# A two-layer hybrid block on one core: the first layer's gates and values in 512-column products, two projections per accumulator in the second, and another order at the beginning

## The chip, the core and the metric

The kernel runs on one core of one Trainium2 chip, in one launch. The metric is device time in microseconds (us), from the start of the program to its end; lower is better. The core has a matrix engine (TensorE, "PE" in the profile, with its weight loads as "PEld"), a vector engine (VectorE, "DVE"), an engine for functions and copies (ScalarE, "ACT"), GpSimd ("POOL") and SyncE ("SP"), from whose queue the loads are issued.

## The reference, cut to what matters

There are 512 latent tokens and 256 context tokens of width 1024, and two layers. Each layer normalises and modulates the tokens, projects them by one wide matrix, and feeds three mixers: a gated linear attention with 4 heads, a gated recurrence with 8 heads, and a windowed attention with 8 query heads. Each mixer has its own SiLU gate. The second layer doesn't update the context, so its queries, gates and merging are needed for the 512 latent tokens alone.

```python
h  = _rms_norm(x, norm_g) * (1.0 + scale) + shift
hc = _rms_norm(ctx, norm_g) * (1.0 + scale_c) + shift_c
(ga_q, ga_k, ga_v, ga_g, ga_lr, hg_q, hg_f, hg_i, hg_g,
 wa_q, wa_k, wa_v, wa_g, mg) = _split_in(jnp.matmul(h, w_in))
...
y_gla = _head_norm_gate(o_gla, gla_norm_g, ga_g)          # ... * silu(ga_g)
y_hg  = _head_norm_gate(o_hg, hgrn_norm_g, hg_g)          # ... * silu(hg_g)
y_att = _window_attention(q, k, v, kc, vc, attn_sink) * jax.nn.silu(wa_g)
x_new = x + gate * _merge((y_gla, y_hg, y_att), mg, w_branch, w_out)
```

## The kernel before, in words

**Data.** Activations stand transposed: 8 chunks of 128 channels (`k` or `kt`) by 768 tokens, the 512 latent ones first (`NL`), then the 256 of the context (`NC`); `NT` is 768. Every fp32 value that a projection reads is held as a rounded part and a rest, `hH[k]` and `hL[k]` for the activations, `WH(i)` and `WL(i)` for a weight block of 128 columns, which lies in a ring of three (`wring`). A projection is the sum of three products per chunk: WH by hH, WH by hL, WL by hH. Each is one matmul instruction, so 8 chunks make 24 matmuls per output piece.

**Projections.** `proj_T` (line 801) gives channels by tokens: 24 matmuls of 512 columns for the latent tokens and, where the context is wanted too, 24 of 256 columns. `proj_V` (line 819) gives tokens by channels for two weight blocks at once: six groups of 128 tokens, 24 matmuls of 256 columns each. Both write an accumulator that `acc()` (line 623) hands out: 128 partitions by 1024 fp32 words, of which there are two, used in turn. A new accumulator can be written when the readers of the one before the last are done. `silu_evac` (line 1339) reads a gate's 768 (or 512) columns with one SiLU on ScalarE; values are copied out 768 columns at a time by ScalarE or VectorE.

**Order.** The program is written out engine by engine by a generator. A plan lists the projections (`make_plan`), and between their matmuls `pace()` (line 694) puts in steps of background work: the recurrences (`rec_head`) and the attention (`att_block`) of heads whose projections are done. Which step comes when is decided by the generator's own running estimate of each engine's time. Background products go to four smaller accumulators (`mx`). Each engine has its instructions in one written order; semaphores join the engines. Most instructions are issued in helpers, so a row's line is the helper's: L533 is a matmul, L549 a transpose by TensorE, L545 a matmul of 32 output rows, L439 an ACT function, L481 and L479 copies on ACT and DVE, L450 a DVE two-operand operation, L466 a DVE operation with a scalar.

**The beginning.** In the first layer (l = 0) `j_start` makes `h` chunk by chunk while the first two projections run. For chunk k there are: `cond_mm(k)` (8 matmuls of 32 output rows that give shift and scale), `cond_cols(k)` (small products on TensorE that turn them into columns, then two small DVE operations), `make_h1(k)` (two DVE operations, then ACT writes `hH[k]`), and `make_h2(k)` (two DVE operations that write `hL[k]`). Round k of the loop issues, in this order: `make_h2(k)`, the first projection's six matmuls, `cond_mm(k + 2)`, the second projection's six, `cond_cols(k + 2)`, `make_h1(k + 2)`, and from round 3 on `split_v()`, which prepares weights of the next projection on ACT and DVE.

Of the kernel before, what the change touches and what calls it, by code (L numbers as in the profile page):

```python
# [18 lines left out]
F32R = mybir.dt.float32r  # L19
# [300 lines left out]
class Emit:  # L320
# [104 lines left out]
    def act(self, out, in_, func, bias=None, scale=None, accum_out=None):  # L425
        want = None
        if func in (AF.Exp, AF.Ln):
            want = COMBINED
        elif func in (AF.Silu, AF.Sigmoid):
            want = str(func)  # L430
        self.table(want)
        kw = {}
        if bias is not None:
            kw['bias'] = bias
        if scale is not None:
            kw['scale'] = scale
        if accum_out is not None:
            kw['accum_out'] = accum_out
        self.nc.scalar.activation(out, in_, func, **kw)  # L439
        self._do('a', 0.833 * self.size(out) + 95 + (90 if accum_out is not None else 0), out, [in_, bias, scale])  # L440
        if accum_out is not None:
            self.written[accum_out.tensor.name] = self.t['a']
            self.writer[accum_out.tensor.name] = 'a'


    def tt(self, out, a, b, op, eng='v'):
        n = self.size(out)
        cost = {'v': 1.04 * n + 65, 'g': 2.25 * n + 100}
        e = eng if eng in cost else self._pick(cost, out, [a, b])
        (self.nc.vector if e == 'v' else self.nc.gpsimd).tensor_tensor(out, a, b, op=op)  # L450
        self._do(e, cost[e], out, [a, b])
# [80 lines left out]
    def mm(self, out, lhsT, rhs, start=True, stop=True):  # L532
        self.nc.tensor.matmul(out, lhsT=lhsT, rhs=rhs, start=start, stop=stop)  # L533
        n = self.size(rhs)
        if rhs.dtype == F32:
            cost = max(1.667 * n + 6, 224)
        elif rhs.dtype == BF16:
            cost = 60
        else:
            cost = max(0.4167 * n + 13.5, 107 if self.size(lhsT) > 64 else 60)  # L540
        self._do('pe', cost, out, [lhsT, rhs])
# [17 lines left out]
def build(nc, tc, A, COL, es, dump=None):  # L559
# [7 lines left out]
    mx_p = es.enter_context(tc.tile_pool(name="mx", bufs=4, space=PSUM))  # L567

    spool = es.enter_context(tc.tile_pool(name="slots", bufs=NSLOT))
    hH = [pool.tile([P, NT], F32R, name=f"hH{k}") for k in range(KT)]  # L570
    hL = [pool.tile([P, NT], F32R, name=f"hL{k}") for k in range(KT)]
    wring = pool.tile([P, NS, 2, KT, P], F32R, name="wring")
    raw_p = es.enter_context(tc.tile_pool(name="raw", bufs=NRAW))
    ncols = A['cols'].shape[1]
# [35 lines left out]
    def ps_tile(kind, p, shape, n):  # L610
        t = p.tile(shape, F32, tag=kind, name=kind)
        names = live[kind]
        if len(names) >= n:
            old = min(names, key=lambda x: E.seq.get(x, 0))
            E.free_at[t.tensor.name] = E.used.get(old, 0.0) + E.FREE
            names.remove(old)
        names.append(t.tensor.name)
        return t

    def mx():  # L620
        return ps_tile('mx', mx_p, [P, 512], 4)

    def acc():
        return ps_tile('acc', acc_p, [P, 1024], 2)


    queue = arena.queue = deque()
# [66 lines left out]
    def pace(slack=SLACK):  # L694
        while max(E.t['v'], E.t['a']) < E.t['pe'] + slack:
            b = first(E.t['pe'] + 50)
            if b is None:
                break
            step(b)
# [81 lines left out]
    def take(n=1):  # L781
        i = pos[0]
        for j in range(at_job[0], i):
            ring_free[j % NS] = E.t['pe'] + E.FREE
        at_job[0] = i
        pos[0] += n
        loads()
        splits(i + n)
        return i
# [5 lines left out]
    def WH(i):  # L795
        return wring[:, i % NS, 1]

    def WL(i):
        return wring[:, i % NS, 0]

    def proj_T(i, xH, xL, ctx, m=P):

        ps = acc()
        E.t['pe'] = max(E.t['pe'], wready[i])
        for t0, n in ((0, NL), (NL, NC)) if ctx else ((0, NL),):
            k = 0
            for kt in range(KT):
                for w, x in ((WH(i), xH), (WH(i), xL), (WL(i), xH)):
                    mm(ps[0:m, t0:t0 + n], w[:, kt, 0:m], x[kt][:, t0:t0 + n],
                       start=(k == 0), stop=(k == 3 * KT - 1))  # L810
                    k += 1
                if kt == 1 and t0 == 0:
                    ahead()
                if kt % 2 == 1:
                    pace()
        pace()
        return ps

    def proj_V(i, evac):

        s = i % NS
        E.t['pe'] = max(E.t['pe'], wready[i + 1])
        wh = wring[:, s:s + 2, 1]
        wl = wring[:, s:s + 2, 0]
        for t in range(6):
            if t % 3 == 0:
                ps = acc()
            k = 0
            for kt in range(KT):
                for x, w in ((hH, wh), (hL, wh), (hH, wl)):  # L830
                    mm(ps[:, 256 * (t % 3):256 * (t % 3 + 1)],
                       x[kt][:, P * t:P * (t + 1)], w[:, :, kt, :],
                       start=(k == 0), stop=(k == 3 * KT - 1))
                    k += 1
            if t == 0:
                ahead()
            if t % 3 == 2:
                evac(t // 3, ps)
            pace()


# [99 lines left out]
    def make_h2(l, k, x, parts=(0, 1)):  # L941

        for j in parts:
            sl = slice(PARTS[j][0], sum(PARTS[j]))
            stt(hL[k][:, sl], x.ap[:, sl], ada[l][:, k, j:j + 1], hH[k][:, sl].bitcast(F32), ALU.add, ALU.subtract)
        if 1 in parts:
            x.free()
# [388 lines left out]
        finish()  # L1336


    def silu_evac(ps, n):
        b = arena.alloc(n)  # L1340
        act(b.ap, ps[:, 0:n], AF.Silu)
        return b

    def tok(bufs, w, c, o=0, r=False):
        b = bufs[c // 3]
        return (b.r if r else b.ap)[:, 256 * (c % 3) + o:256 * (c % 3) + o + w]
# [28 lines left out]
    def j_start(l, arg):  # L1375
# [36 lines left out]
        def cond_mm(k):  # L1412


            w = stage[k]
            ps = mx()
            for kt in range(KT):
                j = kt % 4
                E.mm4(ps[32 * j:32 * j + 32, 0:2 * P], cs32[:, kt], w[kt // 3].ap[:, 256 * (kt % 3):256 * (kt % 3 + 1)],
                      start=(kt < 4), stop=(kt >= 4))  # L1420
            stage[k] = r = arena.alloc(NT)
            copy(r.ap[:, 0:2 * P], ps[:, 0:2 * P], eng='va', psum=True)
            for b in w:
                b.free()
# [38 lines left out]
        def products(kt, of=(0, 1), js=(0, 1)):  # L1463
            E.t['pe'] = max(E.t['pe'], wready[i + 1])
            for j in js:
                for w, x in ((WH(i + j), hH), (WH(i + j), hL), (WL(i + j), hH)):
                    for t0, n in parts[j]:
                        if (t0 > 0) not in of:
                            continue
                        c = count[j][t0 > 0]  # L1470
                        mm(ps[j][:, t0:t0 + n], w[:, kt], x[kt][:, t0:t0 + n], start=(c == 0), stop=(c == 3 * KT - 1))
                        count[j][t0 > 0] += 1

        count = [[0, 0], [0, 0]]
        if l == 0:

            for k in range(KT):
                make_h2(l, k, xs[k])
                if k == 1:
                    load_rest()  # L1480
                if k == KT - 1:
                    ahead()
                products(k, js=(0,))
                if k + 2 < KT:
                    cond_mm(k + 2)
                products(k, js=(1,))
                if k + 2 < KT:
                    cond_cols(k + 2)
                    make_h1(l, k + 2, xs[k + 2], rs)
                if k >= 3 and raw_v:  # L1490
                    split_v()
        else:

            tail = S0.pop('tail')
            for part in range(2):
                make_h1(l, 0, xs[0], rs, (part,))
                if part == 0:
                    tail[0]()
                for k in range(KT):
                    if k + 1 < KT:  # L1500
                        make_h1(l, k + 1, xs[k + 1], rs, (part,))
                    make_h2(l, k, xs[k], (part,))
                    if part and k == KT - 1:
                        ahead()
                    products(k, (part,))
                    if part == 0 and k in (0, 2):
                        tail[1 + k // 2]()
# [63 lines left out]

    def j_v(l, h):
        S_['v'][h] = vb = [arena.alloc(NT) for _ in range(2)]
        proj_V(take(2), lambda j, ps: copy(vb[j].ap, ps[:, 0:NT], eng='va', psum=True))

    def j_gq(l, h):
        ps = proj_T(take(), hH, hL, S_['ctx'])
# [1 line left out]
        act(qb.ap, ps[:, 0:S_['nt']], AF.Copy, scale=float(128 ** -0.5))  # L1579

    def j_g(l, key):
        ps = proj_T(take(), hH, hL, S_['ctx'])
        S_['g'][key] = silu_evac(ps, S_['nt'])

    def j_grun(l, h):
        q, k, vb = S_['q'].pop(h), S_['k'].pop(h), S_['v'].pop(h)
# [272 lines left out]
```

## Time and profile before

| | |
|---|---|
| median of 3 runs | 2699.06 us (2696.78 to 2701.8) |
| the profiled execution: time | 2699.6 us |
| the profiled execution: span, first to last instruction | 2697.8 us |
| TensorE busy | 2617.0 us, 97% of the span |
| weight loads, VectorE, ScalarE, GpSimd busy | 86%, 66%, 41%, 6% |
| mean granted TensorE clock | 0.991 of full speed |
| DMA | 227.68 MB, 84 GB/s over the span |

TensorE is busy nearly all the time, so its own instructions and the few places where it waits make the time. What the other engines do counts only where TensorE waits for them.

### The profile page before, as it was taken

How to read it: one execution, taken by the hardware profiler on the slowest of the kernel's cores; microseconds unless marked ns; L12 is line 12 of the kernel's file. 1: busy time of each engine (PE TensorE's matmuls, PEld its weight loads, DVE VectorE, ACT ScalarE, POOL GpSimd, SP SyncE). 2: the span in 40 equal slices, each digit the busy share in tenths (PEclk: the TensorE clock that was granted, in tenths of full speed). 3: DMA queues.
4: the chain of work that ended last, by engine and by line, in shares of the span. 5: the costliest groups of instructions: out<-in, count | busy, mean ns of one | idle time of the engine just before them, and what ended most of it. 6: DMA issues, size and time to landing. Idle time of an engine off the chain costs nothing. (4 is left out here: it accounts for less than half of the span.)

```text
span 2697.8 us, 40579 instructions
## 1 busy us (share of the span) xinstructions
PE 2617.0 (97%) x15982; PEld 2318.4 (86%) x15982; DVE 1767.1 (66%) x3592; ACT 1105.6 (41%) x2037; POOL 168.9 (6%) x426
## 2 busy tenths in 40 slices
PE   6999999999999999999999999999999999999998
PEld 3899988999888889888888898888899797888886
DVE  4466666786877766775556556667887887765454
ACT  3444434443434455411111344444665545563222
POOL 0000002010020100000000000001011110000000
PEclk8999999999999999999999999999999999999999
DMA  6111121111121112463423411112221122224333
GB/s 251 40 50 57 59 67 59 50 52 57 49 66 50 46 57 74 148 204 101 140 95 102 141 55 56 62 63 63 69 65 62 55 75 73 73 87 142 126 125 109
DMA packets 89342, 227.68 MB, mean 84 GB/s; under 512 B 9920, under 2 KB 30912, under 8 KB 89152
## 3 DMA queue, kind: packets, MB, share of 16 engines
q1 hardware_dynamic: 89152, 225.09, 25.3%
q8 instruction: 126, 2.06, 0.3%
q14 instruction: 64, 0.52, 0.1%
HBM read 202.24 MB, written 22.81 MB: 83 GB/s over the span
## 5 line engine op out<-in xcount | busy, mean ns | idle before, releaser
L533 PE MATMUL acc<-hH,wring 128*128 128x512 f32 (+1 forms) x5040 | 1402.9, 357 | 14.9 <-ACT s L439 9.8
L533 PEld LDWEIGHTS acc<-hH,wring 128*128 128x128 f32 x5040 | 897.7, 190 | 143.1 <-ACT s L439 11.6
L533 PE MATMUL acc<-hL,wring 128*128 128x512 f32 (+1 forms) x2520 | 884.8, 352 | 16.9 <-DVE hL L466 16.8
L533 PEld LDWEIGHTS acc<-hL,wring 128*128 128x128 f32 x2520 | 479.1, 190 | 76.9 <-DVE hL L466 20.5
L533 PE MATMUL mx<-s,s 128*128 128x256 f32 (+4 forms) x2576 | 389.5, 299 | 12.9 <-DVE s L513 4.4
L533 PEld LDWEIGHTS mx<-s,s 128*128 128x128 f32 (+1 forms) x2576 | 348.4, 192 | 32.8 <-issue 7.1
L450 DVE TENSOR_TENSOR wring<-raw,wring 128x1024 fp32r<-128x1024 f32 x269 | 330.7, 1235 | 28.2 <-ACT wring L481 19.3
L533 PE MATMUL acc<-s,wring 128*128 128x512 f32 (+1 forms) x1728 | 332.4, 354 | 0.5 <-DVE s L450 0.5
L533 PEld LDWEIGHTS acc<-s,wring 128*128 128x128 f32 x1728 | 285.6, 189 | 46.4 <-DVE s L450 0.9
L439 ACT ACTIVATE s<-s 128x768 f32<-128x768 f32 (+1 forms) x321 | 259.0, 816 | 129.8 <-DVE s L466 83.1
L481 ACT CAST wring<-raw 128x1024 fp32r<-128x1024 f32 x173 | 179.7, 1048 | 276.9 <-PE acc L533 182.9
L533 PE MATMUL acc<-wring,hH 128*128 128x256 f32 x1536 | 286.1, 285 | 0.0
L450 DVE TENSOR_TENSOR s<-s,s 128x768 f32<-128x768 f32 (+5 forms) x279 | 234.0, 855 | 67.0 <-ACT s L439 45.9
L533 PEld LDWEIGHTS acc<-wring,hH 128*128 128x128 f32 x1536 | 242.2, 192 | 0.3
L533 PE MATMUL acc<-wring,hL 128*128 128x256 f32 x768 | 217.2, 283 | 0.0
L450 DVE TENSOR_TENSOR s<-s,fb 128x128 f32<-128x128 f32 (+2 forms) x608 | 183.0, 361 | 0.8
L439 ACT ACTIVATE s<-acc 128x768 f32<-128x768 f32 (+2 forms) x112 | 76.3, 683 | 255.9 <-PE acc L533 236.2
L481 ACT COPY s<-mx 128x256 f32<-128x256 f32 (+2 forms) x190 | 67.4, 379 | 225.8 <-PE mx L533 142.8
L479 DVE CAST wring<-raw 128x1024 fp32r<-128x1024 f32 x103 | 71.6, 695 | 117.5 <-PE acc L533 114.4
L533 PEld LDWEIGHTS acc<-wring,hL 128*128 128x128 f32 x768 | 147.3, 192 | 0.2
L481 ACT COPY s<-acc 128x768 f32<-128x768 f32 (+2 forms) x129 | 87.8, 681 | 101.0 <-PE acc L533 98.9
L549 PE MATMUL mx<-const,s 128*128 128x128 f32 (+1 forms) x732 | 109.1, 275 | 15.7 <-DVE s L450 14.6
(112 smaller groups left out, 2144.8 us busy)
## 6 DMA issues: line engine op xcount, KB each, us to landing
raw<-in_W SPq DMA_DIRECT2D x308, 512.0 KB, 3.8
y<-s SPq DMA_DIRECT2D x80, 128.0 KB, 1.7
s<-y SPq DMA_DIRECT2D x24, 384.0 KB, 6.1
s<-in_xT SPq DMA_DIRECT2D x16, 384.0 KB, 4.0
s<-in_wada SPq DMA_DIRECT2D x16, 384.0 KB, 7.6
s<-y SPq DMA_DIRECT2D x24, 256.0 KB, 4.4
y<-s SPq DMA_DIRECT2D x80, 64.0 KB, 1.6
s<-in_wvl SPq DMA_DIRECT2D x8, 288.0 KB, 6.2
```

The costliest lines, as they stand in the source:

```text
L439: self.nc.scalar.activation(out, in_, func, **kw)
L450: (self.nc.vector if e == 'v' else self.nc.gpsimd).tensor_tensor(out, a, b, op=op)
L479: self.nc.vector.tensor_copy(out, in_)
L481: self.nc.scalar.copy(out, in_)
L533: self.nc.tensor.matmul(out, lhsT=lhsT, rhs=rhs, start=start, stop=stop)
L549: self.nc.tensor.transpose(out, in_, ident)
```

## The change

It has four parts.

1. **Gates of the first layer, context part.** `hH[k]` and `hL[k]` become the two halves of one tile. For the 256 context tokens a gate's projection (24 of them: 8 for each mixer) multiplies WH by both halves in one matmul of 512 columns, and WL by hH in one of 256 columns that adds to the second half of the output. The two halves of the output are added on reading: ACT copies one, DVE adds the other, and SiLU then runs as one call of 512 columns out of the accumulator and one of 256 columns in place.
2. **Values of the first layer.** `proj_V2` does the same for the seven value projections that go by `j_v`: per group of 128 tokens and chunk one matmul of 512 columns (hH by WL and WH of both blocks) and one of 256 (hL by WH). Each of six groups is read by a copy on ACT and an addition on DVE; an accumulator holds two groups, where it held three.
3. **Projections of 512 tokens alone** (all of them in the second layer) take half an accumulator, so two of them share one.
4. **The beginning.** `make_h2(k + 1)` is issued in round k, behind `cond_mm(k + 2)`, ahead of `cond_cols(k + 2)` and `make_h1(k + 2)`.

```diff
-    hH = [pool.tile([P, NT], F32R, name=f"hH{k}") for k in range(KT)]
-    hL = [pool.tile([P, NT], F32R, name=f"hL{k}") for k in range(KT)]
+    hHL = [pool.tile([P, 2, NT], F32R, name=f"h{k}") for k in range(KT)]
+    hH, hL = ([t[:, j] for t in hHL] for j in range(2))
...
+    half = [None, 0]
     def acc():
+        half[1] += 1
         return ps_tile('acc', acc_p, [P, 1024], 2)
+    def acc_bank():
+        t = half[0]
+        if t is not None and half[1] < 2:
+            half[0] = None
+            return t
+        t = acc()
+        half[:] = t[:, NL:2 * NL], 0
+        return t[:, 0:NL]
...
+    def psum2(out, a, b):
+        copy(out, a, eng='a', psum=True)
+        tt(out, out, b, ALU.add)
-    def proj_T(i, xH, xL, ctx, m=P):
-        ps = acc()
+    def proj_T(i, xH, xL, ctx, xHL=None):
+        ps = acc() if ctx else acc_bank()
...
+                if t0 and xHL:
+                    todo = [(ps[:, NL:], WH(i), xHL[kt][:, :, NL:NT]), (ps[:, NT:], WL(i), xH[kt][:, NL:NT])]
+                    todo = todo[::1 if kt < KT - 1 else -1]
...
+    def proj_V2(i, out):
...
+        for t in range(6):
+            if t % 2 == 0:
+                ps = acc()
+            o = 512 * (t % 2)
+            lo, hi = ps[:, o:o + 256], ps[:, o + 256:o + 512]
+            for kt in range(KT):
+                todo = [(ps[:, o:o + 512], hH, w[:, :, :, kt].rearrange("p s h c -> p h s c")), (hi, hL, w[:, :, 1, kt])]
...
+            psum2(out[t // 3].ap[:, 256 * (t % 3):256 * (t % 3 + 1)], lo, hi)
...
+            make_h2(l, 0, xs[0])
             for k in range(KT):
-                make_h2(l, k, xs[k])
...
                 products(k, js=(0,))
                 if k + 2 < KT:
                     cond_mm(k + 2)
+                if k + 1 < KT:
+                    make_h2(l, k + 1, xs[k + 1])
                 products(k, js=(1,))
...
-        ps = proj_T(take(), hH, hL, S_['ctx'])
-        S_['g'][key] = silu_evac(ps, S_['nt'])
+        nt = S_['nt']
+        ps = proj_T(take(), hH, hL, S_['ctx'], hHL)
+        S_['g'][key] = b = arena.alloc(nt)
+        if nt > NL:
+            psum2(b.ap[:, NL:NT], ps[:, NL:NT], ps[:, NT:])
+        for t0, n in ((0, NL), (NL, NC))[:1 if nt == NL else 2]:
+            act(b.ap[:, t0:t0 + n], (b.ap if t0 else ps)[:, t0:t0 + n], AF.Silu)
```

In the program as built, TensorE has 14,399 instructions where it had 14,927 (528 fewer), ACT has 66 more copies of 256 columns out of an accumulator, 13 fewer of 768 columns and 123 table loads where it had 104, and DVE has 66 more additions of 256 columns out of an accumulator.

The first place is VectorE's order in rounds 0 and 1 of the beginning, before. `hL_78` and `hL_79` are chunks 1 and 2 of the rests, `hH_70` and `hH_71` the rounded parts that they are taken from, `ada` and `amod` the columns that `cond_cols` gives, and the operations on `s_112` and `s_113` are `make_h1` of chunks 2 and 3.

```order
L450 TENSOR_TENSOR ada_100<-mx,cols 128x2x2
L466 SCALAR_TENSOR_TENSOR amod_102<-ada_100,cols 128x2
L466 SCALAR_TENSOR_TENSOR s_112<-s_112,amod_102,s_265 128x512
L466 SCALAR_TENSOR_TENSOR s_112<-s_112,amod_102,s_265 128x256
L466 SCALAR_TENSOR_TENSOR hL_78<-s_111,ada_100,hH_70 128x512
L466 SCALAR_TENSOR_TENSOR hL_78<-s_111,ada_100,hH_70 128x256
L450 TENSOR_TENSOR ada_100<-mx,cols 128x2x2
L466 SCALAR_TENSOR_TENSOR amod_102<-ada_100,cols 128x2
L466 SCALAR_TENSOR_TENSOR s_113<-s_113,amod_102,s_265 128x512
L466 SCALAR_TENSOR_TENSOR s_113<-s_113,amod_102,s_265 128x256
L466 SCALAR_TENSOR_TENSOR hL_79<-s_112,ada_100,hH_71 128x512
L466 SCALAR_TENSOR_TENSOR hL_79<-s_112,ada_100,hH_71 128x256
```

The same place on VectorE in the change; the tiles are now `h_70` and `h_71` for both halves, and `s_104` and `s_105` are the same inputs under other numbers.

```order
L466 SCALAR_TENSOR_TENSOR h_70<-s_103,ada_92,h_70 128x512
L466 SCALAR_TENSOR_TENSOR h_70<-s_103,ada_92,h_70 128x256
L450 TENSOR_TENSOR ada_92<-mx,cols 128x2x2
L466 SCALAR_TENSOR_TENSOR amod_94<-ada_92,cols 128x2
L466 SCALAR_TENSOR_TENSOR s_104<-s_104,amod_94,s_257 128x512
L466 SCALAR_TENSOR_TENSOR s_104<-s_104,amod_94,s_257 128x256
L479 COPY s_370<-mx 128x256
L466 SCALAR_TENSOR_TENSOR h_71<-s_104,ada_92,h_71 128x512
L466 SCALAR_TENSOR_TENSOR h_71<-s_104,ada_92,h_71 128x256
L450 TENSOR_TENSOR ada_92<-mx,cols 128x2x2
L466 SCALAR_TENSOR_TENSOR amod_94<-ada_92,cols 128x2
```

The rest of chunk k + 1 stood behind the columns and the `make_h1` of chunk k + 2; now it stands ahead of them, and behind the copy of `cond_mm` where that copy is VectorE's.

The second place is ScalarE's order at the first gate of the first layer, before: the SiLU out of the accumulator, a weight block's cast, and the background's exponentials and logarithms, with the loads of function tables between them.

```order
L439 ACT_TABLE_LOAD
L439 ACTIVATE s_825<-acc 128x768
L481 CAST wring<-raw_757 128x1024
L439 ACTIVATE s_847<-s_827 128x768
L421 ACT_TABLE_LOAD
L439 ACTIVATE s_847<-s_847 128x768 x2
```

The same place on ScalarE in the change.

```order
L481 COPY s_809<-acc 128x256
L439 ACT_TABLE_LOAD
L439 ACTIVATE s_809<-acc 128x512
L439 ACTIVATE s_809<-s_809 128x256
L439 ACTIVATE s_834<-s_814 128x768
L421 ACT_TABLE_LOAD
```

One ACT instruction became three, and the last of them reads what VectorE adds to the copy.

The third place is TensorE in the attention of the second layer, where one query projection ends and the next begins, before; here the numbers tell accumulators apart.

```order
L533 MATMUL acc_20500<-hH7_76,wring_85 128x512
L533 MATMUL acc_20500<-hL7_84,wring_85 128x512
L533 MATMUL acc_20500<-hH7_76,wring_85 128x512
L533 MATMUL acc_20612<-hH0_69,wring_85 128x512
L533 MATMUL acc_20612<-hL0_77,wring_85 128x512
L533 MATMUL acc_20612<-hH0_69,wring_85 128x512
```

The same two projections on TensorE in the change.

```order
L533 MATMUL acc_20093<-h6_75,wring_77 128x512 x3
L533 MATMUL acc_20093<-h7_76,wring_77 128x512 x3
L549 MATMUL mx_20168<-const_82,s1015_20025 128x128 x2
L533 MATMUL acc_20093<-h0_69,wring_77 128x512 x3
L533 MATMUL acc_20093<-h1_70,wring_77 128x512 x3
```

The second projection goes on in the accumulator of the first, in its other half, so a new one is taken with every second projection.

## Rows read from the trace of the kernel before

**Rows 1.** The page: span, and TensorE's busy time, share and instructions.

```profile
span 2697.8 us, 40579 instructions
...
PE 2617.0 (97%) x15982; PEld 2318.4 (86%) x15982; DVE 1767.1 (66%) x3592; ACT 1105.6 (41%) x2037; POOL 168.9 (6%) x426
```

**Rows 2.** TensorE's waits by what ended them: us in total, times, longest.

```profile
PE acc L533 <- DVE hL L466: 16.8, 8, 3.0
...
PE acc L533 <- ACT s L439: 9.8, 4, 3.9
...
PE acc L533 <- ACT s L481: 3.0, 2, 1.6
...
PE acc L533 <- DVE s L466: 1.8, 1, 1.8
```

**Rows 3.** Busy time by stretch: length, PE, PEld, DVE, ACT, POOL, granted clock, DMA.

```profile
22.30:76.65 54.35, 37.98 (x219) 24.51 (x219) 26.32 (x58) 13.44 (x25) 0.00 (x0) 0.81 0.50 180
24.71:28.12 3.41, 3.38 (x20) 1.62 (x20) 0.38 (x1) 0.08 (x1) 0.00 (x0) 0.50 1.04 397
76.65:1130.00 1053.35, 1035.68 (x6893) 946.96 (x6892) 708.22 (x1551) 468.35 (x951) 89.56 (x218) 1.00 0.19 59
2085.00:2460.00 375.00, 357.63 (x2111) 309.46 (x2110) 272.08 (x586) 206.44 (x437) 26.01 (x43) 0.99 0.24 77
```

**Rows 4.** Timeline of the beginning, 21 to 47 us: start, us, engine, [idle before <-releaser].

```profile
23.66 1.12 ACT L439 ACTIVATE hH<-s,ada 128x512 fp32r<-128x512 f32 x2 [1.46 <-DVE s L466]
...
29.35 0.50 PE L533 MATMUL mx<-const,s 128*128 128x2 f32 x4
...
30.28 1.15 DVE L466 SCALAR_TENSOR_TENSOR s<-s,amod,s 128x512 f32<-128x512 f32 x2
...
31.07 1.12 ACT L439 ACTIVATE hH<-s,ada 128x512 fp32r<-128x512 f32 x2 [2.37 <-DVE s L466]
31.35 1.14 DVE L466 SCALAR_TENSOR_TENSOR hL<-s,ada,hH 128x512 fp32r<-128x512 f32 x2
...
32.15 0.78 PE L533 MATMUL acc<-hL,wring 128*128 128x512 f32 x2 [1.84 <-DVE hL L466]
```

**Rows 5.** Timeline of TensorE, 1000 to 1030 us: triples of matmuls at both widths.

```profile
1002.16 0.28 PE L533 MATMUL acc<-hL,wring 128*128 128x256 f32 x1
...
1003.96 0.28 PE L533 MATMUL acc<-hL,wring 128*128 128x256 f32 x1
...
1006.49 0.39 PE L533 MATMUL acc<-hL,wring 128*128 128x512 f32 x1
...
1007.85 0.39 PE L533 MATMUL acc<-hL,wring 128*128 128x512 f32 x1
```

**Rows 6.** Groups on ScalarE by shape: busy us, mean ns | idle before.

```profile
L439 ACT ACT_TABLE_LOAD x53 | 68.0, 1283 | 5.0 <-PE acc L533 3.4 <-PEq L1844 0.7
...
L439 ACT ACTIVATE s<-acc 128x768 f32<-128x768 f32 x52 | 42.3, 813 | 178.5 <-PE acc L533 178.4
L439 ACT ACTIVATE s<-acc 128x512 f32<-128x512 f32 x52 | 31.0, 599 | 58.3 <-PE acc L533 57.8
...
L481 ACT COPY s<-acc 128x256 f32<-128x256 f32 x10 | 3.7, 373 | 37.4 <-PE acc L533 36.1 <-DVE s L479 1.3
```

**Rows 7.** The same on VectorE.

```profile
L450 DVE TENSOR_TENSOR s<-mx,s 128x256 fp32r<-128x256 f32 x48 | 19.5, 421 | 1.2
```

**Rows 8.** Timeline of TensorE at three waits for an accumulator.

```profile
1123.53 0.57 PE L533 MATMUL acc<-hH,wring 128*128 128x512 f32 x1 [2.87 <-ACT s L439]
...
2110.46 0.50 PE L533 MATMUL acc<-hH,wring 128*128 128x512 f32 x1 [1.31 <-ACT s L481]
...
2284.40 0.79 PE L533 MATMUL acc<-hH,wring 128*128 128x512 f32 x1 [3.95 <-ACT s L439]
```

**Rows 9.** Timeline of ScalarE ahead of the last of these waits.

```profile
2278.62 0.29 ACT L439 ACTIVATE sm<-nsink,sm 128x1 f32<-128x1 f32 x1 [8.58 <-DVE sm L450]
...
2283.75 1.09 ACT L439 ACTIVATE s<-acc 128x512 f32<-128x512 f32 x2
```

More of the change, by code (lines that the diff above doesn't have):

```diff
@@ L799, in WL @@
         return wring[:, i % NS, 0]
-    def proj_T(i, xH, xL, ctx, m=P):
-        ps = acc()
+    def psum2(out, a, b):
[3 more added lines that the diff above has]
+        ps = acc() if ctx else acc_bank()
         E.t['pe'] = max(E.t['pe'], wready[i])
         for t0, n in ((0, NL), (NL, NC)) if ctx else ((0, NL),):
-            k = 0
             for kt in range(KT):
[L808 to L811, printed above, removed]
+                if t0 and xHL:
+                    todo = [(ps[:, NL:], WH(i), xHL[kt][:, :, NL:NT]), (ps[:, NT:], WL(i), xH[kt][:, NL:NT])]
+                    todo = todo[::1 if kt < KT - 1 else -1]
+                else:
+                    todo = [(ps[:, t0:t0 + n], w, x[kt][:, t0:t0 + n])
+                            for w, x in ((WH(i), xH), (WH(i), xL), (WL(i), xH))]
+                for k, (o, w, x) in enumerate(todo):
+                    mm(o, w[:, kt], x, start=(kt == 0 and k == 0), stop=(kt == KT - 1 and k == len(todo) - 1))
                 if kt == 1 and t0 == 0:
@@ L838, in proj_V @@
                 evac(t // 3, ps)
+            pace()
+    def proj_V2(i, out):
+        s = i % NS
+        E.t['pe'] = max(E.t['pe'], wready[i + 1])
+        w = wring[:, s:s + 2]
+        for t in range(6):
[5 more added lines that the diff above has]
+                todo = [(ps[:, o:o + 512], hH, w[:, :, :, kt].rearrange("p s h c -> p h s c")), (hi, hL, w[:, :, 1, kt])]
+                for k, (a, x, r) in enumerate(todo[::1 if kt < KT - 1 else -1]):
+                    mm(a, x[kt][:, P * t:P * (t + 1)], r, start=(kt == 0 and k == 0), stop=(kt == KT - 1 and k == 1))
+            if t == 0:
+                ahead()
+            psum2(out[t // 3].ap[:, 256 * (t % 3):256 * (t % 3 + 1)], lo, hi)
             pace()
@@ L1336, in att_block @@
         finish()
[L1339 to L1342, printed above, removed]
     def tok(bufs, w, c, o=0, r=False):
@@ L1573, in j_v @@
         S_['v'][h] = vb = [arena.alloc(NT) for _ in range(2)]
-        proj_V(take(2), lambda j, ps: copy(vb[j].ap, ps[:, 0:NT], eng='va', psum=True))
+        if l == 0:
+            proj_V2(take(2), vb)
+        else:
+            proj_V(take(2), lambda j, ps: copy(vb[j].ap, ps[:, 0:NT], eng='va', psum=True))
     def j_gq(l, h):
```

## The prediction

> **What bounds the kernel now.** I read the page first, then who TensorE waited for, then the stretches, and the timeline last. TensorE is busy for 2617.0 of 2697.8 us [rows 1], so the time is its instructions, some 2617, and some 80 of waiting. The list of its waits shows where these lie: the largest entry, 16.8 us in eight waits, is for `hL`; 9.8, 3.0 and 1.8 are for accumulators that ACT or VectorE had not yet read [rows 2]; the rest are small ones for the background. By stretch, the waits for `hL` are nearly all in the beginning: of the 54.35 us from the first projection's start to its end TensorE is busy for 37.98 and idle for 16.4, with a mean granted clock of 0.81; in the rest of the first layer it is idle for 17.7 of 1053 at a clock of 1.00 [rows 3]. VectorE (708 of 1053) and ACT (468) have room there. So a gain must come from fewer or shorter TensorE instructions, or from those waits, and what the other engines are given matters only where TensorE then waits for it.
>
> **The beginning.** The timeline shows a round. The rounded part of chunk 1 was written by ACT from 23.66 to 24.78, and only `hL` was missing. But VectorE stood at chunk 2's columns, which need TensorE's product at 29.35; then came `make_h1` at 30.28 and `hL` at 31.35; TensorE, waiting for it, went on at 32.15 after 1.84 idle [rows 4]. So each round ended with TensorE waiting for work that could have been done five microseconds earlier. The new order puts it earlier. Seven waits make up the 16.4; the first, for chunk 0, keeps its place and I leave it its 1.84. That removes 14.5.
>
> What is late next is the chain that is left: columns at 29.35, `make_h1`, `hH` from 31.07 to 32.19, then 1.14 for `hL` [rows 4]. Counted from the end of the columns' products (29.7), that is 3.6 us into the round that follows, and `hL` is wanted when that round is over. At full clock the work of the stretch is about 30 us (below); the last two rounds, without `cond_mm`, are six matmuls of 512 columns and six of 256, which is 2.1 us at the rates of [rows 5]; so the first six last about (30 - 4.2) / 6 = 4.3. The chain fits in those, barely from round 3 on, when `split_v` puts a cast and a subtraction ahead of it, and it doesn't fit in round 6: there `hL` of chunk 7 comes 1.5 late. I charge 2 us in all (bounds 0 and 5): 12.5 gained.
>
> The clock comes on top. A mean of 0.81 over 54.35 us, with 1.2 and 2.4 GHz as the levels, is 20.7 us at the lower one. One such stretch, 24.71 to 28.12, follows the first wait, with TensorE at work through it [rows 3]; it stays. In the other 17.2 us TensorE did at half speed what it can do in half the time: 8.6 if it was busy throughout. I take 8, because in the first layer's other thousand microseconds, where waits are short, the clock is at 1.00 (bounds 0 and 8.6). The beginning gives 20.5.
>
> **Products of 512 columns.** Five triples of 256 columns take 1003.96 - 1002.16 = 1.80 us, so 120 ns each; two triples of 512 take 1007.85 - 1006.49 = 1.36, so 227 each [rows 5]. The 256 more columns cost 107, so 13 ns of each instruction don't depend on its columns. Three of 256 (360 ns) become one of 512 and one of 256 (347): 13 ns saved. There are 24 gates x 8 chunks and 7 values x 6 groups x 8 chunks, together 528 triples: 6.9 us, all on the engine that bounds. Nothing in the trace has a 512-column product whose columns lie in pieces, as the new ones do (two pieces for a gate, four for values), so the bounds are 0 and 6.9. A rule of the Trainium skill speaks against this term: its page "TensorE: Matmul & The Clock Gate", section "Wait — 56ns, not 53.3ns?", has matmuls start N columns / 2.4 GHz + about 2.5 ns apart. By it the triples would save 2.5 x 528 = 1.3 us, an estimate from that page, and the sum would be 2674; the trace, with 120 and 227, doesn't agree.
>
> **Two projections per accumulator.** Of the waits for accumulators 2.87 at 1123.5 is in the first layer, where they are still taken whole. The others are in the second layer's attention: 9.8 - 2.87 = 7.0 behind ACT functions, 1.31 of the 3.0 behind ACT copies at 2110.5 (the other is in the layer's first projections), and 1.8 behind VectorE [rows 2, 8]. Together 10.1 us. The largest shows why: ACT stood still for 8.58 us until VectorE gave it the softmax's numbers at 2278.6, with the gate's SiLU queued behind it until 2283.75, and TensorE, two projections on, waited 3.95 [rows 8, 9]. With halves a new accumulator is taken with every second projection and waits for readers of at least two projections ago, twice 24 x 227 ns or 11 us, in place of one. That covers all these waits. But the background's order is decided anew, and ACT and VectorE are as late as before, so some of this will come back as waits for background products. I take 6 of 10, and 1 for the clock, whose mean is 0.99 in this stretch [rows 3]: 7 us (bounds 0 and 13).
>
> **What reading the halves costs.** ACT gets 66 copies of 373 ns (24.6 us), 19 table loads of 1283 (24.4) and, per gate, 599 and about 410 for the split SiLU in place of 813 (4.8 in all), less 13 copies of 768 columns at about 800: some 43 us more. VectorE gets 66 additions of about 421: 28 us [rows 6, 7]. In the first layer ACT has 585 us of idle time and VectorE 345 [rows 3], which is what hides it. If that cover is gone, it shows in one way: VectorE's addition waits for ACT's copy with all of VectorE's queue behind it, the gate's last SiLU waits for the addition with ACT's queue behind it, and the accumulator, now with three readers, comes free late. A wait of that kind costs 2.87 at its worst in the first layer now [rows 8]. I charge one more of these, 3 us (bounds 0 and 15, twelve table loads of 1.28 all on the path).
>
> **The sum.** 20.5 + 6.9 + 7 - 3 = 31.4. The profiled execution took 2699.6 for a span of 2697.8, and stands 0.5 above the median of 2699.06, so 2699.6 - 31.4 = **2668 us**. All terms at their good ends give 14.5 + 8.6 + 6.9 + 13 = 43, so 2657.
>
> **The rivals.**
> - *The waits only move.* TensorE runs ahead of ACT and VectorE in the second layer and stops at a background product instead, and the first layer's new chain costs 8 in place of 3. For it: all five waits are at places where another engine was late, and halves don't make it earlier. Against it: VectorE is busy for 272 of the 375 us there and ACT for 206 [rows 3], so both can catch up. Time: 2699.6 - 20.5 - 6.9 + 8 = 2680.
> - *The clock stays low in the beginning.* For it: small products with 32 output rows remain in every round, and the one wait that stays is followed by the lower level. Against it: the waits go. Time: 2668 + 8 = 2676.
> - *The products save nothing.* The 13 ns may go with each piece of the columns, and the number of pieces is the same before and after. For it: no row shows a 512-column product in pieces. Against it: the cost is a constant of the instruction at both widths. Time: 2668 + 7 = 2675. The Trainium skill's rule named above comes out nearly here.
> - *Slower.* Each of 24 gates and 21 value accumulators is read through ACT, VectorE and, for gates, ACT again. If each keeps TensorE waiting, the gain is gone. To end 0.2% above the time before, this must cost 31 + 5 + the 3 already charged, over 45 readings 0.9 us each. For it: ACT once waited 8.58 for VectorE [rows 9]. Against it: a gate's accumulator has at least one whole projection, 24 x (227 + 120) ns = 8.3 us, until it is wanted. Time: 2706.
>
> **How the numbers follow.** The forecast has 0.60, and by itself lies between 2657 and 2677. The waits that move have 0.18, the low clock 0.10, the products that save nothing 0.05, slower 0.04; 0.03 is left for more than I count. The range reaches from just below all good ends to above the first rival with a wait or two more: 2654 to 2686. A measurement of this kernel tells about 0.2% (5.4 us) from no change, so faster means under 2693.7: all cases but the last, less the tail of the first rival: 0.93 faster, 0.03 the same, 0.04 slower.
>
> **What would show it.** The beginning: the first projections end near 56 us instead of 76.65, with waits for `hL` of 1.84 and one of 1 to 2, and a clock above 0.9 in the stretch. The products: triples 347 ns apart, 15,454 matmul records. The accumulators: no wait for one in the second layer's attention. Wrong would be a wait for `hL` in every round, new waits of TensorE for accumulators in the first layer, or waits for background products in the second that add up to what the accumulators lost.

## The result, and the profile after

The changed kernel takes **2847.0 us** (median of 4 runs, 2843.1 to 2852.1) against 2698.3 for the kernel before: a ratio of 1.055, 95% interval 1.053 to 1.057. The prediction was 2668. It is slower by 149 us where 31 less were forecast.

The page of the changed kernel, its span, TensorE's row and the granted clock by slices:

```profile
span 2844.9 us, 39623 instructions
...
PE 2653.9 (93%) x15454; PEld 2310.0 (81%) x15454; DVE 1792.8 (63%) x3660; ACT 1140.1 (40%) x2127; POOL 172.4 (6%) x429
...
PEclk9999999999999999999999999999999989889999
```

TensorE's busy time, which should have fallen, grew from 2617.0 [rows 1] to 2653.9, and its share fell to 93%: it waits more, and it runs more slowly. The list of its waits says for whom (line of the waiter, releaser; us in total, times, longest):

```profile
PE acc L533 <- ACT s L439: 50.8, 19, 7.7
PE acc L533 <- DVE s L450: 37.6, 25, 5.8
PE acc L533 <- DVE s L466: 24.2, 8, 9.1
PE acc L533 <- ACT s L481: 13.4, 3, 7.1
PE acc L533 <- DVE s L479: 13.3, 4, 6.7
PE mx L549 <- DVE s L450: 11.8, 14, 1.6
PE acc L533 <- ACT wring L481: 7.0, 8, 0.9
```

The waits for `hL` that led this list [rows 2] are gone. In their place stand accumulators: in the first three rows and the fifth TensorE wants to write `acc` while ACT or VectorE, by an instruction on the line named, still has to read a part of it. The fourth is mostly two waits for a branch's input (4.7 and 7.1 us). The last names a cast of weights, but its 0.9 us stand at every second projection near the end, and the list of before has no such row. In the program as built, at one of them, the instruction just ahead of the matmul waits for VectorE's read of the accumulator's first half, and the cast that the matmul itself waits for was done two projections earlier: that is a wait for an accumulator too. By stretch (length; busy PE, PEld, DVE, ACT, POOL; granted clock; DMA share, GB/s):

```profile
22.40:54.78 32.38, 29.86 (x220) 20.79 (x220) 24.86 (x55) 12.51 (x24) 0.00 (x0) 0.95 0.79 287
...
54.78:1130.00 1075.22, 1032.03 (x6336) 915.87 (x6336) 722.43 (x1600) 484.44 (x1024) 96.01 (x222) 0.99 0.18 55
1553.69:2085.00 531.31, 514.56 (x3230) 463.91 (x3231) 366.92 (x717) 267.47 (x437) 45.75 (x143) 0.99 0.19 58
2085.00:2460.00 375.00, 315.17 (x1748) 271.24 (x1747) 232.67 (x484) 168.32 (x340) 25.32 (x56) 0.91 0.19 60
2460.00:2844.90 384.90, 330.20 (x1503) 266.04 (x1501) 177.61 (x279) 114.68 (x193) 5.08 (x4) 0.95 0.30 99
```

The beginning did what was forecast: 32.4 us where it took 54.35 at a clock of 0.81 [rows 3], with 2.5 of idle time in place of 16.4. From 54.78 to 1130 TensorE now idles for 43 us (17.7 from 76.65 to 1130 before). In 2085 to 2460, the second layer's attention, it idles for 60 of 375 where it idled for 17 [rows 3], and the clock fell from 0.99 to 0.91. The second layer as a whole, from its first projection to the end, went from 1159.7 us (1538.1 to 2697.8) to 1291.2 (1553.7 to 2844.9). That is 131.5 of the 147 that the span grew; of it 93.7 are TensorE's gaps over 0.15 us (27.3 to 121.0) and 37.8 the same matmuls running longer (6,476 records in both, 1121.7 and 1159.5 us from start to start).

**Second halves.** The plainest place is the timeline near the end, where nothing else disturbs (start, us, engine, operation, count, [idle before <-releaser]):

```profile
2639.75 5.15 PE L533 MATMUL acc<-h,wring 128*128 128x512 f32 x22
2645.59 11.17 PE L533 MATMUL acc<-h,wring 128*128 128x512 f32 x48 [0.69 <-ACT s L439]
2657.45 5.73 PE L533 MATMUL acc<-h,wring 128*128 128x512 f32 x24 [0.69 <-ACT s L439]
...
2644.94 0.60 ACT L439 ACTIVATE s<-acc 128x512 f32<-128x512 f32 x1 [4.61 <-PE acc L533]
...
2656.80 0.60 ACT L439 ACTIVATE s<-acc 128x512 f32<-128x512 f32 x1 [3.46 <-PE acc L533]
```

The projection of a merging weight (`mg` in the reference) ends, ACT reads it by one sigmoid from 2644.94, and only then, at 2645.59, does TensorE start the next projection, though that one goes to the other half of the accumulator. Then 48 matmuls, two projections, run through; then again 0.69 us. So a second half waits for the reader of the first half, which is the projection just before: nothing is left to hide the read. Before, such projections ran through one after the other, as these branch products, more than seven projections in one row, where the changed kernel stops for some 0.8 us at every second one:

```profile
2469.82 40.28 PE L533 MATMUL acc<-s,wring 128*128 128x512 f32 x177
```

The program as built says why; these are TensorE's rows for the accumulator at 2657.45, first the first half's start, then the second's, and the count of ACT's semaphore that the second waits for is the one that its read of the first half gives:

```
8307 L533 MATMUL acc_22578<-h0_69,wring_77 128x512 [waits DVE_49]
...
8317 L533 MATMUL acc_22578<-h0_69,wring_77 128x512 [waits Activation_49]
```

Here it costs 0.69, since ACT is idle and reads at once. In the attention ACT is late, and the wait is as long as its queue:

```profile
2181.97 0.30 ACT L439 ACTIVATE ss<-ss,eps 128x2 f32<-128x2 f32 x1
...
2186.76 0.37 ACT L439 ACTIVATE fb<-fb 128x204 f32<-128x204 f32 x1 [4.26 <-POOL fb L483]
2187.15 1.28 ACT L439 ACT_TABLE_LOAD   x1
...
2188.45 0.60 ACT L439 ACTIVATE s<-acc 128x512 f32<-128x512 f32 x1
...
2189.10 3.35 PE L533 MATMUL acc<-h,wring 128*128 128x512 f32 x7 [7.73 <-ACT s L439]
```

ACT stood for 4.26 us behind GpSimd's numbers for a recurrence, then loaded a table, then read the projection (a merging weight's again). Before, a projection stood between a read and the write that waits for it, 24 x 227 ns or some 5.5 us, an estimate from [rows 5].

**The clock.** What follows that wait is shown by three stretches of the changed kernel: the seven matmuls right behind it, a stretch without waits, and one with waits of 4.9 us (begun before it), 9.1 and 5.0. The last two rows are the whole second layer, of the changed kernel and then of the kernel before.

```profile
2189.10:2192.45 3.35, 3.35 (x8) 2.67 (x9) 0.42 (x1) 0.00 (x0) 0.00 (x0) 0.50 0.70 221
2200.00:2240.00 40.00, 40.00 (x298) 37.89 (x298) 31.13 (x69) 20.18 (x39) 6.10 (x17) 1.00 0.24 78
2400.00:2460.00 60.00, 43.32 (x207) 36.66 (x208) 27.90 (x55) 21.60 (x43) 2.35 (x1) 0.80 0.16 48
...
1553.69:2844.90 1291.21, 1159.93 (x6476) 1001.19 (x6476) 777.20 (x1479) 550.47 (x969) 76.15 (x203) 0.96 0.23 71
...
1538.13:2697.80 1159.67, 1121.75 (x6476) 981.65 (x6476) 775.44 (x1480) 539.53 (x960) 79.12 (x204) 0.99 0.24 79
```

Behind the wait TensorE is at 0.50, the lower of its two levels (1.2 GHz), and works through 3.35 us of matmuls at half speed; without waits it is at 1.00 (2.4 GHz). Over the second layer the trace has 112.5 us at the lower level where it had 20.9, and matmuls at work in 76.4 of them where it was 13.6. What these would have taken at the upper level is half of it, so the clock cost 38.2 us in place of 6.8: an estimate that explains 31 of the 38. So the waits are in part paid a second time.

**Values.** Of the 37.6 us behind VectorE's L450 33.8 lie in the first layer, in 20 waits, and these are value projections. One of them:

```profile
92.25 1.28 ACT L439 ACT_TABLE_LOAD   x1
...
98.12 1.03 ACT L481 CAST wring<-raw 128x1024 fp32r<-128x1024 f32 x1
99.05 0.36 ACT L481 COPY s<-acc 128x256 f32<-128x256 f32 x1
...
99.18 1.22 DVE L450 TENSOR_TENSOR wring<-raw,wring 128x1024 fp32r<-128x1024 f32 x1
100.32 0.41 DVE L450 TENSOR_TENSOR s<-s,acc 128x256 f32<-128x256 f32 x1
...
100.79 7.38 PE L533 MATMUL acc<-wring,h 128*128 128x512 f32 x32 [5.82 <-DVE s L450]
```

The first group's sum is copied by ACT at 99.05 and finished by VectorE at 100.32, behind the weights' subtraction, and TensorE, which wants the second group's half of the same accumulator, has stood for 5.82 us.

### The profile page after: what moved, and what is told of

Read it like the earlier page. It is cut to its first block, busy times and chain, and to the rows that moved or that the text cites. A ratio compares the mean times of both kernels' runs of the same rounds, so it can differ in the third digit from the quotient of the medians.

```text
span 2844.9 us, 39623 instructions
## 1 busy us (share of the span) xinstructions
PE 2653.9 (93%) x15454; PEld 2310.0 (81%) x15454; DVE 1792.8 (63%) x3660; ACT 1140.1 (40%) x2127; POOL 172.4 (6%) x429
## 5 line engine op out<-in xcount | busy, mean ns | idle before, releaser
L533 PE MATMUL acc<-h,wring 128*128 128x512 f32 (+1 forms) x7368 | 1539.2, 364 | 93.4 <-ACT s L439 50.8
L533 PEld LDWEIGHTS acc<-h,wring 128*128 128x128 f32 x7368 | 1229.6, 192 | 299.7 <-ACT s L439 57.5
L450 DVE TENSOR_TENSOR wring<-raw,wring 128x1024 fp32r<-128x1024 f32 x269 | 330.0, 1232 | 37.0 <-ACT wring L481 28.4
L533 PE MATMUL acc<-wring,h 128*128 128x256 f32 (+1 forms) x1968 | 292.5, 308 | 33.4 <-DVE s L450 33.4
L439 ACT ACTIVATE s<-s 128x768 f32<-128x768 f32 (+2 forms) x345 | 268.5, 788 | 130.6 <-DVE s L466 87.9
L533 PEld LDWEIGHTS acc<-wring,h 128*128 128x128 f32 x1968 | 265.2, 193 | 54.5 <-DVE s L450 39.0
L450 DVE TENSOR_TENSOR s<-s,s 128x768 f32<-128x768 f32 (+4 forms) x276 | 232.3, 858 | 64.0 <-ACT s L439 41.8
L450 DVE TENSOR_TENSOR s<-s,acc 128x256 f32<-128x256 f32 (+2 forms) x114 | 66.7, 586 | 204.9 <-PE acc L533 133.8
L481 ACT COPY s<-acc 128x256 f32<-128x256 f32 (+2 forms) x186 | 103.9, 559 | 210.2 <-PE acc L533 206.5
L450 DVE TENSOR_TENSOR s<-s,fb 128x128 f32<-128x128 f32 (+2 forms) x606 | 180.5, 357 | 0.7
L439 ACT ACTIVATE s<-acc 128x512 f32<-128x512 f32 (+2 forms) x112 | 71.3, 637 | 214.9 <-PE acc L533 182.2
L479 DVE CAST wring<-raw 128x1024 fp32r<-128x1024 f32 x109 | 75.5, 693 | 84.1 <-PE acc L533 83.1
L450 DVE TENSOR_TENSOR s<-mx,ss 128x256 f32<-128x256 f32 (+1 forms) x60 | 30.8, 513 | 135.1 <-ACT ss L439 135.0
L450 DVE TENSOR_TENSOR s<-mx,s 128x128 f32<-128x128 f32 (+3 forms) x188 | 77.9, 445 | 56.1 <-PE mx L533 36.8
L549 PEld LDWEIGHTS mx<-const,s 128*128 128x128 f32 (+1 forms) x732 | 87.0, 141 | 27.7 <-issue 9.2
```

Of the source, the lines that this page charges most:

```text
L479: self.nc.vector.tensor_copy(out, in_)
L481: self.nc.scalar.copy(out, in_)
L549: self.nc.tensor.transpose(out, in_, ident)
```

## The experiments

Two theories were set against each other. **Halves**: a matmul into the second half of an accumulator waits for the first half's readers. **Load**: ACT and VectorE have 43 and 28 us more to do, with 19 more table loads, and are late for that reason. Each run is timed beside the kernel before, whose medians in these comparisons lay between 2698 and 2702; a median of another run that differs by under some 3 us is not told apart by its ratio alone.

### Whole accumulators again

```diff
-        ps = acc() if ctx else acc_bank()
+        ps = acc()
```

> The changed kernel with part 3 undone: every projection takes a whole accumulator again. Theory (halves): a matmul into the second half of an accumulator waits for the readers of the first half, which are those of the projection just before. Then the second layer should take its 1160 us of before in place of 1291, and the time is 2847 - 131 = about 2716, with the values' waits (38 us behind VectorE's additions) still there. Rival (load): TensorE waits because ACT and VectorE have 43 and 28 us more to do and 19 more table loads. All of that stays, so the time stays above 2800.

Measured: 2714.7 us, ratio 1.005 (1.004 to 1.006). The second layer takes 1159.4 us, as before. TensorE's waits:

```profile
PE acc L533 <- DVE s L450: 34.2, 20, 5.8
...
PE acc L533 <- ACT s L481: 8.3, 3, 5.3
PE acc L533 <- ACT s L439: 7.0, 3, 4.0
```

The row of 50.8 is down to 7.0, that behind L479 is gone, that behind L466 is down to one wait of 1.8, and the values' row stays. All the added work of ACT and VectorE is still there: load can't have been the cause in the second layer.

### Halves alone

The kernel before with `acc_bank()` and its one use in `proj_T`, and nothing else.

> The kernel before with part 3 alone. Theory (halves): about 2698 + 131 = 2829, with waits for accumulators of 0.7 to 9 us at every second projection of the second layer. Rival (load): ACT and VectorE have nothing added here, so at most a few us, under 2710, as the prediction had it (2691).

Measured: 2832.4 us, ratio 1.048 (1.047 to 1.050). In the second layer the list of waits is that of the changed kernel nearly to the tenth:

```profile
PE acc L533 <- ACT s L439: 50.8, 19, 7.7
PE acc L533 <- DVE s L466: 23.9, 8, 9.1
PE acc L533 <- DVE s L479: 13.0, 4, 6.7
PE acc L533 <- ACT s L481: 8.5, 2, 6.9
PE acc L533 <- ACT wring L481: 7.0, 8, 0.9
```

Part 3 costs 131 us by itself (beside 2701.7 of the kernel before in this comparison).

### Halves spread over two accumulators

Is it the second half as such, or the neighbour read just before? Here projections go to the first half of one accumulator, the first of the other, the second of the one, the second of the other.

```diff
-    half = [None, 0]
+    spare, made, last = [], [0], [None]
     def acc():
-        half[1] += 1
+        last[0] = made[0]
+        made[0] += 1
...
-        t = half[0]
-        if t is not None and half[1] < 2:
-            half[0] = None
+        spare[:] = [x for x in spare if x[0] >= made[0] - 2]
+        if spare and spare[0][0] != last[0]:
+            last[0], t = spare.pop(0)
             return t
         t = acc()
-        half[:] = t[:, NL:2 * NL], 0
+        spare.append((last[0], t[:, NL:2 * NL]))
         return t[:, 0:NL]
```

> The changed kernel with halves given out in another order: two accumulators are live, and projections go to the first halves of both, then to the second halves of both, so a second half's neighbour was read one projection earlier. Theory (a second half waits for the readers of the first): these readers then have a projection's time, as before, so the time comes near the run with whole accumulators, 2715, plus up to 20 where whole accumulators of layer 2 stand between halves. Rival (working in the second half costs something by itself): it stays at 2847.

Measured: 2721.6 us, ratio 1.008 (1.007 to 1.010), with the early read of the values still in it. The waits behind L439 fall to 7.6 us, and near the end, where each second projection waited 0.69, four run through:

```profile
2531.45 21.92 PE L533 MATMUL acc<-h,wring 128*128 128x512 f32 x96
```

Its second layer takes 1167.5 us, 8 more than with whole accumulators, so the write into a second half isn't what costs the 131. What costs is that the whole accumulator is one thing to wait for, and that its other half was read a moment ago.

### Four small accumulators

The idea of part 3, done so that nothing is shared: the kernel before with part 4, and from the second layer's attention on the space of the two accumulators is given out as four of 512 words.

```diff
+    acc_n = [acc_p, 1024, 2]
...
+    def four():
+        acc_es.close()
+        acc_n[:] = acc_es.enter_context(tc.tile_pool(name="acc4", bufs=4, space=PSUM)), 512, 4
+        live['acc'] = []
...
     def j_aq(l, h):
+        if l == 1 and h == 0:
+            four()
```

> The kernel before with part 4, and from the second layer's attention on four accumulators of 512 words of their own in place of two of 1024 (what part 3 was taken for in the prediction: a new one waits for readers of three projections ago). If that idea holds, the 10 us of waits for accumulators in the attention go, and by the prediction's term (7) 2677 - 7 = 2670. Rival (the waits only move): ACT and VectorE are as late as before, TensorE stops at background products instead, and the time is 2677.

Measured: 2672.4 us, ratio 0.990 (0.989 to 0.991), where the beginning alone (below) has 2677.4. The intervals of these two ratios overlap; the traces have 1155.5 us for the second layer against 1160.0. Of the second layer's waits for accumulators

```profile
PE acc L533 <- DVE s L450: 5.2, 2, 4.7
PE acc L533 <- ACT s L481: 3.0, 2, 1.6
...
PE acc L533 <- ACT s L439: 2.3, 1, 2.3
```

the 3.95 and the one behind L466 went, and a new one of 4.7 behind VectorE's L450 came. So in the traces halves that are independent are worth 4.5 us, not far from the 7 of the prediction; the times by themselves don't show it. The Trainium skill, "PSUM — Partial Sum Buffer", section "PSUM bank collisions raise a hardware error", asks for guards by bank and quadrant, and 512 words of fp32 are by its section "Specifications (TRN2)" a whole bank, so that two halves need no guard against each other. This run, with the same space in four pieces, agrees: the wait was the built program's, not the chip's.

### Values read late

As whole accumulators, and both groups of an accumulator are read after the second.

```diff
-            psum2(out[t // 3].ap[:, 256 * (t % 3):256 * (t % 3 + 1)], lo, hi)
+            if t % 2 == 1:
+                for j in (t - 1, t):
+                    o = 512 * (j % 2)
+                    psum2(out[j // 3].ap[:, 256 * (j % 3):256 * (j % 3 + 1)], ps[:, o:o + 256], ps[:, o + 256:o + 512])
```

> As the run with whole accumulators, and the two groups of values in an accumulator are both read after the second, in place of each after its own. Theory (halves): the 25 waits behind VectorE's additions (37.6 us) go, less a few that come back behind the accumulator, so about 2716 - 33 = 2683, faster than the kernel before. Rival (load): the same copies, additions and table loads are there, so the same time as with the early read, 2716.

Measured: 2684.4 us, ratio 0.994 (0.993 to 0.995). The row behind L450 went from 34.2 us to

```profile
PE acc L533 <- DVE s L450: 1.5, 2, 1.0
```

with the same copies, additions and table loads. The reading was not too much work but too early: 30 us.

### The beginning alone

The kernel before with part 4 only (the two hunks of the diff at `make_h2`).

> The kernel before with part 4 alone. By the prediction's term 2698 - 20.5 = 2678, and the first projections end near 56 us. Rival: the later work, whose background order is decided anew, gives part of it back, 2688 or more.

Measured: 2677.4 us, ratio 0.991 (0.990 to 0.992), so 24 under the kernel before beside it; the profiled span is 2676.8 against 2697.8, and the second layer begins 21.3 us earlier. All of the gain is kept.

### Gates, and values, beside the beginning

The run with late values without part 2, and without part 1.

> The kernel before with parts 4 and 1 (beginning and gates), whole accumulators. Beside the beginning alone (2677.4): by the prediction's term 192 triples x 13 ns give 2.5 us, so 2675. By the trace of the run with late values, where the gates' products of 512 columns took 245 ns on average and saved nothing, 2678. Rival (readings): ACT's and VectorE's added readings keep TensorE waiting, 2681 or more.

> The kernel before with part 4 and part 2 with the late read (both groups after the second), whole accumulators, gates as before. Beside the beginning alone (2677.4): by the prediction's term 336 triples x 13 ns, so 2673. By the trace of the run with late values (2.4 us saved in the products) 2675. Rival (readings): 42 copies and 42 additions more keep TensorE waiting and 2681 or more comes out. The run with gates and late values together was 7 us above the beginning alone: if the parts add, the two differences sum to 7; if the background's new order makes them, they needn't.

Measured: gates 2683.2 us, ratio 0.994 (0.993 to 0.995); values 2677.9, ratio 0.993 (0.991 to 0.994). In the traces, taken from each matmul's start to the next one's and without gaps over 0.15 us, the gates' wider products save 2.3 us and the values' 1.9; a triple is 235 + 117 ns for both (medians). The gates' products therefore gave nearly what was forecast, and yet the run is 5.8 above the beginning alone, values 0.5. The timeline of its first layer's end has one wait that the beginning alone doesn't have:

```profile
1114.70 0.83 ACT L481 CAST s<-s 128x768 fp32r<-128x768 f32 x1 [7.50 <-DMA s<-y]
...
1115.58 0.79 PE L533 MATMUL acc<-s,wring 128*128 128x512 f32 x1 [5.67 <-ACT s L481]
```

ACT waits for the load of a branch's input, TensorE for ACT. The branch products behind it ran slower, 134.8 us for the same 576 against 131.2.

### Gates except the attention's

```diff
-                hg=j_g, ..., ag=j_g, ...
+                hg=j_g, ..., ag=lambda l, h: j_g(l, h, False), ...
```

(`False` keeps the old products and the one SiLU for the attention's 8 gates of the first layer.)

> The beginning and the gates, but the attention's 8 gates of the first layer as before, so 16 of 24 are changed. If the gates' loss of 5.8 us lies in their readings (copy, addition, second SiLU), two thirds of it stay: 2677.4 + 3.9 = 2681. If it is the single wait of 5.7 us at the end of the first layer, where a branch's input is loaded late because the attention's last block came later, it goes with the attention's gates: 2677.4 - 16 x 8 x 12 ns = 2676.

Measured: 2675.4 us, ratio 0.991 (0.990 to 0.993); of its six executions two took 2681.3 and 2682.6, the others 2674.0 to 2675.8. In the trace the wait is gone, and by the median 16 gates read through copy, addition and two SiLUs cost nothing. So the loss comes with the attention's gates. It isn't always that one wait: the run with late values has all 24 gates and not this wait, and yet TensorE's gaps over 0.15 us in its first layer (from 57 us on) are 22.6 us where the beginning alone has 17.0, the longest in this row:

```profile
PE mx L549 <- DVE s L462: 5.4, 4, 3.5
```

By which step of the background's new order the attention's gates make such waits stays open.

### Together

All four parts with both mends; the same without the gates; the beginning, 16 gates and four small accumulators.

> All four parts, with the two mends: values read late, and from the second layer's attention on four accumulators of 512 words. By the runs with late values (2684.4) and with four small accumulators (5.0 under the beginning alone): 2684.4 - 5.0 = 2679. If the added readings and the small accumulators disturb each other in the second layer, 2684 or more.

> The beginning, values with the late read and four small accumulators; gates as before. By sums: 2677.9 - 5.0 = 2673, no more than a measurement's noise from the run with four small accumulators alone (2672.4), so the values' products are worth nothing. Were the 1.9 us that the products save in the trace kept, 2670.

> The beginning, 16 of the 24 gates and four small accumulators; values and the attention's gates as before. By sums of the runs: 2675.4 - 5.0 = 2670, which would be the fastest of all. If the background's order, decided anew once more, costs what the parts give, 2673 or more.

Measured: 2680.2 (ratio 0.992, 0.991 to 0.994), 2672.3 (0.989, 0.988 to 0.990) and 2672.6 us (0.990, 0.989 to 0.992). The first two came as the sums say. The third should have been 2670 and was not: no version is measurably faster than the beginning with four small accumulators, which beats the kernel before by 1.0%.

## Why the prediction was wrong

- **The step that failed** is in "Two projections per accumulator": "With halves a new accumulator is taken with every second projection and waits for readers of at least two projections ago". True of the first half, and nothing was said of the second. It is written while its accumulator's first half is being read, and the built program waits there. A term of -7 (bounds 0 and 13) became +131 (halves alone), in the changed kernel 131.5 in the second layer's length. A little of it isn't second halves themselves but what they delay, as the branch's input at 7.1 us. The rows for it were not in the trace of before: no accumulator was written there after a part of it had been read, since all groups were read after the last. So the bound should have had a bad side: every second projection waits for a read with no cover, from 0.7 us to as long as the 3.95 of [rows 8] plus the projection that covered it.
- **What reading the halves costs** was +3 (bounds 0 and 15). It was 37.3, the run with whole accumulators against the beginning alone, or 41.5 with the products' gain added. The mechanism was named ("VectorE's addition waits for ACT's copy ... and the accumulator comes free late"), but the cover was taken to be a whole projection. For values it was the same failed step: the next group wants the neighbouring half at once. Read late, 30 of the 37 are gone; the other 7 come close to what gates (5.8) and values (0.5) cost beside the beginning alone.
- **The beginning**, -20.5: measured 21 by the spans, 24 by the medians. First projections ended at 54.8 (forecast 56), with waits for `hL` of 1.84 and 0.68, and the clock was 0.95. Both halves of the term came out: 13.9 us less idle time (12.5 forecast) and 8.1 less busy time (8 forecast for the clock).
- **Products**, -6.9: 2.3 + 1.9. For gates right (2.5), for values 1.9 of 4.4. The rival that they save nothing holds in time for the values (2677.9 against 2677.4).
- **The rivals.** "Slower" had the sign, and 0.04. Its place was half right: it asked 0.9 us of each of 45 readings; the values' second groups paid 1.7 us each on average (33.8 in 20), the gates none. The second layer, where most was lost, was in no rival on that side. The one that the waits only move was wrong about where: in the second layer they weren't at background products but at accumulators, and many more.
- **The sum again**, from separate runs: 2701.7 (before, beside them) - 24.3 (the beginning alone) + 37.3 (gates and early values) + 130.7 (halves alone) = 2845, for a measured 2847.0.

## What to carry to other kernels

When one buffer is cut in two to let work run further ahead, look at what the program waits for: if it waits by buffer and not by the words written, the second part inherits the readers of the first, and the slack becomes shorter than it was. Check it in the built program, at the first instruction that writes the second part, or give each part a buffer of its own, or read both parts only after both are written. And where the trace of before holds no case of "written after partly read", the bound on that step has to include its worst side.

## What the runs showed that was not expected

A wait costs more than its length on TensorE: in the second layer 94 us of added gaps came with 38 us of slower matmuls, some 31 of them by the clock as estimated above, and behind a wait of 7.73 us the next 3.35 us were at a granted clock of 0.50. And a part can save its 2.3 us on the engine that bounds and still end 5.8 us slower: the gates' run has a new wait of 5.67 us, at a load.
